# Operand start offsets for each dense stage, and an SSM decay that is spread through a scratch tensor

## The chip, the cores and the metric

One core of one Trainium2 chip runs the whole kernel. The metric is the device time of one execution in microseconds (us), the median of several executions. The engines are PE (TensorE: matmuls, with PEld as its weight loads), DVE (VectorE), ACT (ScalarE), POOL (GpSimd) and SP (SyncE); POOL and SP only issue transfers here.

## The reference

256 tokens of width 1024 in fp32 go through two blocks. The first has one layer: an input projection, a Mamba-2 (SSM) mixer in chunks of 128 beside a gated linear recurrence (LRU), gates, an output projection and a gated FFN. The second has two layers: a projection, three attention-like mixers and an MLP.

```python
cs = cumsum(dA, chunk axis)                       # dA = dt * A, 32 heads, 2 chunks of 128
lmat = exp(cs_i - cs_j) for i >= j else 0         # within a chunk, per head
y_diag = einsum('bcgls,bcgrls,bcsgrp->bclgrp', C B^T, lmat, x*dt)
decay_states = exp(cs_last - cs)                  # carries chunk 0 into chunk 1
...
h = h + (g_ssm * y_ssm + g_lru * y_lru) @ w_out
h = h + (silu(gate) * up) @ w_ffn_out             # gate, up = rmsnorm(h) @ w_ffn_in
# second block, layer l = 0, 1
x = x + concat(retention, dsa, dilated)(rmsnorm(x) @ w_in) @ w_out
x = x + square(relu(rmsnorm(x) @ w_up)) @ w_down
```

## The kernel before

**Dense stages.** Every weight matrix is streamed from HBM once, in transfers of about 1 MB on SP's queue into `raw` (three buffers). Each piece of 128x1024 numbers is split into an upper part `hi` (ACT, L253) and a rest `lo` (DVE, L254), five buffers of each; `next_piece` asks for splits four pieces ahead of use. The activations are split in the same way into a pair of tiles, and each product is three matmuls that add into one PSUM bank (`mm3`, L330 to L332). In `run_a` the weights are the stationary operand (128 columns) and the activations the moving one (256 columns). `run_b` (L380 to L382) turns this round for a few matrices: activations stationary, 512 (at the end 256) columns of `hi` or `lo` moving. A piece of `run_a` is 24 matmuls.

**The stages, by their activation pair.** `xnh`/`xnl` are one pair of buffers that six stages use in turn: "in" (the input projection, 1848 matmuls), "ffn" (1056), "mix0" (384, and 144 of `run_b`), "up0" (768), "mix1" (384 and 144) and "up1" (768). Inside "in" run the output projections of the SSM (`sTh`/`sTl`, 384), of the LRU (`lTh`/`lTl`, 240) and, after the gates, of the block (`mx0`, `mx1`, 192). The others are `ah`/`al` (FFN output, 528), `mxh`/`mxl` (mixer output, 192 for each of the two layers), `mah0`/`mal0` (MLP output of layer 0, 768) and `mah1`/`mal1` (of layer 1, by `run_b`: 288 of 512 columns, 192 of 256).

**Order.** Side work (SSM, LRU, attention, norms) is written as generators; `tick` runs the next step of one after each pair of output tiles of a dense piece. The recording layer then places the instructions of each engine by its own estimates of time, and each engine runs its list strictly in order.

**The decay.** `dt_task` makes `cs`, the cumulative sums of 32 heads, and its two-part split `csp` (L609, L610). For each pair of heads (16 pairs, four to a group `g`), `bc` broadcasts two rows of `cs` over 128 partitions with two matmuls of 256 columns (L669: `idr` is a stacked identity, one column of it repeated), ACT turns the PSUM bank into decay factors `M` with six 128x128 activations (L674, L676) and one 128x512 exponential (L677), and DVE multiplies by `cbT` (L678). `pvm` then multiplies `M` with the tokens (L688). `M` has two buffers. Around it LRU gates run: `lg_run` fills two `ps_sc` banks by matmul, ACT reads them with sigmoids (L777, L778), and the next two banks can be filled only then.

## Time and profile before

| | |
|---|---|
| median of 3 runs | 1210.4 us (1210.18 to 1211.16) |
| profiled execution, its own time | 1216.44 us |
| its span in the trace | 1214.7 us |
| PE busy | 1202.6 us (99%) |
| DVE busy | 846.8 us (70%) |
| ACT busy | 700.5 us (58%) |
| granted TensorE clock, mean | 0.998 of full speed |

The profiled execution took 6.0 us more than the median, and 1.7 us of its time lie outside the span. Matmuls overlap in the pipeline, so that PE shows busy throughout; what tells is how far apart the matmuls of a stretch start.

### The profile page before, as it was taken

The numbers are of one execution on the slowest core, as the hardware profiler recorded it, in microseconds if no ns is written. First come the engines' busy times: TensorE is split into PE (matmuls) and PEld (weight loads), VectorE is DVE, ScalarE is ACT, GpSimd is POOL, SyncE is SP. The second block draws the span as 40 slices with busy tenths as digits, with TensorE's granted clock in tenths as the row PEclk, the third lists the DMA queues.
The fourth block names the chain that finished last, engine by engine and source line by source line (L and its number), as shares of the span: only waits on it lengthen the run. The fifth ranks groups of instructions, "written<-read, shape, count | busy, mean of one in ns | idle before, by whom it ended". The sixth has DMA issues, their size and how long they took to land.

```text
span 1214.7 us, 22653 instructions
## 1 busy us (share of the span) xinstructions
PE 1202.6 (99%) x9369; PEld 1133.3 (93%) x9369; DVE 846.8 (70%) x1483; ACT 700.5 (58%) x1071; POOL 4.6 (0%) x12
## 2 busy tenths in 40 slices
PE   8999999999999999999999999999999999999997
PEld 8999999999999999999897899999997969999886
DVE  7888988987686666557967586655479586666453
ACT  7698788767466444444546575544355376655342
POOL 0000000000000000000000000000000000000000
PEclk9999999999999999999999999999999999999999
DMA  8455444656555655545353455555554434565550
GB/s 299 135 176 172 151 145 150 206 175 204 196 177 177 197 182 178 185 159 194 121 178 105 138 175 179 196 182 183 169 163 143 134 105 158 185 194 175 192 189 35
DMA packets 109382, 205.21 MB, mean 169 GB/s; under 512 B 5792, under 2 KB 15776, under 8 KB 109152
## 3 DMA queue, kind: packets, MB, share of 16 engines
q1 hardware_dynamic: 108560, 201.09, 50.9%
q0 software_dynamic: 576, 2.62, 0.6%
q8 instruction: 73, 1.20, 0.4%
q14 instruction: 29, 0.24, 0.1%
q10 hardware_dynamic: 144, 0.07, 0.0%
HBM read 202.71 MB, written 1.05 MB: 168 GB/s over the span
## 4 chain that ended last, share of the span: by engine, by line
PE 94%; DVE 4%; ACT 1%; DMA 0%; issue 0%; SPq 0%; ACTq 0%
PE ps_mm L330 25%; PE ps_mm L332 25%; PE ps_mm L331 25%; PE ps_mm L380 3%; PE ps_mm L382 3%; PE ps_mm L381 3%; PE ps_sc L327 2%; PE ps_o L1123 1%; PE ps_o L688 1%; DVE lo L254 1%; DVE acc L1069 1%; PE ps_tp L1110 1%; DVE m L1068 1%; PE ps_sc L669 1%; PE ps_tp L941 0%; DMA xt<-in_x 0%
## 5 line engine op out<-in xcount | busy, mean ns | idle before, releaser
L254 DVE TENSOR_TENSOR lo<-raw,hi 128x1024 fp32r<-128x1024 f32 (+2 forms) x382 | 461.9, 1213 | 284.5 <-ACT hi L253 281.4
L253 ACT ACTIVATE hi<-raw 128x1024 fp32r<-128x1024 f32 (+2 forms) x382 | 400.6, 1053 | 425.9 <-PE ps_mm L331 332.5
L330 PE MATMUL ps_mm<-xnh,hi 128*128 128x256 f32 x1736 | 492.4, 284 | 0.0
L331 PE MATMUL ps_mm<-xnl,hi 128*128 128x256 f32 x1736 | 490.3, 283 | 0.0
L332 PE MATMUL ps_mm<-xnh,lo 128*128 128x256 f32 (+1 forms) x1736 | 489.2, 282 | 0.0
L330 PEld LDWEIGHTS ps_mm<-xnh,hi 128*128 128x128 f32 x1736 | 327.9, 189 | 3.8 <-issue 2.5
L331 PEld LDWEIGHTS ps_mm<-xnl,hi 128*128 128x128 f32 x1736 | 329.2, 190 | 1.3 <-DVE xnl L487 0.2
L332 PEld LDWEIGHTS ps_mm<-xnh,lo 128*128 128x128 f32 (+1 forms) x1736 | 328.2, 189 | 0.4 <-issue 0.2
L330 PE MATMUL ps_mm<-mah,hi 128*128 128x256 f32 x256 | 71.9, 281 | 0.0
L331 PE MATMUL ps_mm<-mal,hi 128*128 128x256 f32 x256 | 71.9, 281 | 0.0
L332 PE MATMUL ps_mm<-mah,lo 128*128 128x256 f32 x256 | 71.9, 281 | 0.0
L382 PE MATMUL ps_mm<-hi,mal 128*128 128x256 f32 (+1 forms) x160 | 56.2, 351 | 0.0
L381 PE MATMUL ps_mm<-lo,mah 128*128 128x256 f32 (+1 forms) x160 | 55.9, 349 | 0.0
L380 PE MATMUL ps_mm<-hi,mah 128*128 128x256 f32 (+1 forms) x160 | 55.7, 348 | 0.0
L330 PE MATMUL ps_mm<-ah,hi 128*128 128x256 f32 x176 | 49.2, 280 | 0.0
L331 PE MATMUL ps_mm<-al,hi 128*128 128x256 f32 x176 | 49.2, 280 | 0.0
L332 PE MATMUL ps_mm<-ah,lo 128*128 128x256 f32 x176 | 49.2, 280 | 0.0
L331 PEld LDWEIGHTS ps_mm<-mal,hi 128*128 128x128 f32 x256 | 49.2, 192 | 0.0
L330 PEld LDWEIGHTS ps_mm<-mah,hi 128*128 128x128 f32 x256 | 48.1, 188 | 0.0
L332 PEld LDWEIGHTS ps_mm<-mah,lo 128*128 128x128 f32 x256 | 48.1, 188 | 0.0
L380 PE MATMUL ps_mm<-hi,xnh 128*128 128x512 f32 x96 | 39.1, 407 | 0.0
L382 PE MATMUL ps_mm<-hi,xnl 128*128 128x512 f32 x96 | 37.8, 394 | 0.0
(384 smaller groups left out, 1885.1 us busy)
## 6 DMA issues: line engine op xcount, KB each, us to landing
raw<-in_w_in SPq DMA_DIRECT2D x61, 1024.0 KB, 5.1
raw<-in_w_up SPq DMA_DIRECT2D x32, 1024.0 KB, 5.4
raw<-in_w_down SPq DMA_DIRECT2D x32, 1024.0 KB, 5.0
raw<-in_w_ffn_in SPq DMA_DIRECT2D x22, 1024.0 KB, 5.2
raw<-in_w_ffn_out SPq DMA_DIRECT2D x10, 1024.0 KB, 5.1
...
raw<-in_w_out SPq DMA_DIRECT2D x16, 512.0 KB, 3.8
...
```

What stands on the lines that cost most here:

```text
L253: S.activation(hi, raw, AF.Copy)
L254: V.tensor_sub(lo, raw, hi.bitcast(F32))
L327: PE.matmul(o, w, x_, start=True, stop=True)
L330: PE.matmul(ps, wh, xh, start=start, stop=False, skip_group_check=True)
L331: PE.matmul(ps, wh, xl, start=False, stop=False, skip_group_check=True)
L332: PE.matmul(ps, wl, xh, start=False, stop=stop, skip_group_check=True)
L380: PE.matmul(o, xh[:, ts], hi[:, k, cs], start=st, stop=False, skip_group_check=True)
L381: PE.matmul(o, xh[:, ts], lo[:, k, cs], start=False, stop=False, skip_group_check=True)
L382: PE.matmul(o, xl[:, ts], hi[:, k, cs], start=False, stop=sp, skip_group_check=True)
L669: PE.matmul(o, idr[:, hh:hh + 1].to_broadcast([64, 128]), csp, start=(i == 0), stop=True, skip_group_check=True)
L688: PE.matmul(ps[64 * i:64 * i + 64, c], xtok[g][:, b, (2 * j + i) * 64:(2 * j + i) * 64 + 64], M[:, i, m], start=(j % 2 == 0 and b == 0), s ...
L1068: V.max(m8, acc[:, a:b])
```

## The change

**Offsets.** Every activation pair is now allocated 32 elements too long (`PAD`), and the data begin at an offset of its own, the same for the upper and the lower tile (`OFF`, in elements of 4 bytes). Before, only `xnh`/`xnl` had offsets (`XOFF`). The address that the allocator gives each tile and this offset together set where the operand starts, modulo 128 bytes. In the built programs the weights `hi` and `lo` start at 32 in both, `sTh`, `lTh`, `mx0`, `mx1` and their lower tiles at 96 in both, and the pairs that the change touches start as follows:

| stage (pair) | before | now |
|---|---|---|
| in (`xnh1`) | 32 | 80 |
| ffn (`xnh3`) | 0 | 88 |
| FFN output (`ah`) | 64 | 88 |
| mix0 (`xnh5`) | 0 | 96 |
| mixer output, both layers (`mxh`) | 32 | 104 |
| up0 (`xnh8`) | 96 | 72 |
| MLP output 0 (`mah0`) | 96 | 80 |
| mix1 (`xnh10`) | 32 | 112 |
| up1 (`xnh13`) | 48 | 104 |
| MLP output 1 (`mah1`, stationary) | 64 | 32 |

**Decay.** `dt_task` writes three rows of `cs` (chunk 1, chunk 0, chunk 1) for all heads into a DRAM tensor `csd` from POOL's queue. `decay_load(q)` reads the 768 numbers of a pair of heads from there into all 128 partitions of `M` (384 KB written). Three loads are issued at once, each later one at the end of a `pvm`; `M` has three buffers. `bc` works on `M` in place. The 32 broadcast matmuls, `idr` and `csp` are gone.

```diff
-XOFF = ((8, 24), (0, 16), (32, 48), (56, 72), (72, 88), (12, 28))
+OFF = {"in": (20, 20), "ffn": (22, 22), "mix0": (24, 24), "up0": (18, 18), "mix1": (28, 28), "up1": (26, 26),
+       "ah": (6, 6), "mx": (18, 18), "mah0": (28, 28), "mah1": (24, 24)}
+PAD = 32
...
+    def pair_tiles(pool, k, stage, names, tags=(None, None)):
+        ab = []
+        for n, t, o in zip(names, tags, OFF[stage]):
+            kw = dict(tag=t) if t else {}
+            tl = pool.tile([128, k * T + PAD], F32R, name=n, **kw)
+            ab.append(tl[:, o:o + k * T].rearrange("p (k t) -> p k t", t=T))
+        return ab
...
+    def decay_load(q):
+        if q < 16:
+            Ms[q] = p1.tile([128, 2, 384], F32, tag="M", bufs=MB, name=f"M{q}")
+            P.dma_start(Ms[q].rearrange("p a b -> p (a b)"),
+                        bass.AP(tensor=csd.tensor, offset=csd.offset + 768 * q, ap=[[0, 128], [1, 768]]))
...
+        for r_, b in enumerate((1, 0, 1)):
+            P.dma_start(csd[:, r_, :], cs[:, b, :])
+        for q in range(MB):
+            decay_load(q)
...
         def bc(j):
-            ps = scb()
-            M = p1.tile([128, 2, 384], F32, tag="M", bufs=2, name=f"M{g}{j}")
+            M = Ms[4 * g + j]
             for i in range(2):
                 hh = 8 * g + 2 * j + i
-                o = ps[:, i * 256:i * 256 + 256]
-                PE.matmul(o, idr[:, hh:hh + 1].to_broadcast([64, 128]), csp, start=(i == 0), stop=True,
-                          skip_group_check=True)
-            for i in range(2):
-                hh = 8 * g + 2 * j + i
-                for r_, src, col in ((0, 128, 1), (128, 0, 0)):
-                    S.activation(M[:, i, r_:r_ + 128], ps[:, i * 256 + src:i * 256 + src + 128], AF.Relu,
+                for r_, col in ((0, 1), (128, 0)):
+                    S.activation(M[:, i, r_:r_ + 128], M[:, i, r_:r_ + 128], AF.Relu,
                                  bias=cst[:, col, hh:hh + 1], scale=-1.0)
-                S.activation(M[:, i, 256:384], ps[:, i * 256 + 128:i * 256 + 256], AF.Exp, bias=cst[:, 2, hh:hh + 1])
+                S.activation(M[:, i, 256:384], M[:, i, 256:384], AF.Exp, bias=cst[:, 2, hh:hh + 1])
...
-        ah = pf.tile([128, 22, T], F32R, name="ah")
-        al = pf.tile([128, 22, T], F32R, name="al")
+        ah, al = pair_tiles(pf, 22, "ah", ("ah", "al"))
```

On PE, between the first two `pvm` of group 0, the rows before were (`ps_o` is `pvm`'s bank, the other rows are the dense stage "in"):

```order
L688 MATMUL ps_o_1367<-M_1252,xtok_1186 64x256 x2
L688 MATMUL ps_o_1367<-M_1252,xtok_1186 64x128 x2
L669 MATMUL ps_sc_1372<-csp,idr 128x256 x2
L330 MATMUL ps_mm_1350<-xnh_118,hi_1170 128x256
L331 MATMUL ps_mm_1350<-xnl_119,hi_1170 128x256
```

At the same place of the changed kernel PE has these (L333 and L334 are the lines that were L330 and L331):

```order
L694 MATMUL ps_o_1365<-M_588,xtok_1192 64x256 x2
L694 MATMUL ps_o_1365<-M_588,xtok_1192 64x128 x2
L333 MATMUL ps_mm_1348<-xnh_120,hi_1176 128x256
L334 MATMUL ps_mm_1348<-xnl_121,hi_1176 128x256
L335 MATMUL ps_mm_1348<-xnh_120,lo_1177 128x256
```

The pair of L669 is gone, as the 15 others are; the dense matmuls around it keep their order.

ACT's list before, early in "in", where it splits weights (L253) and evacuates the first LRU tiles (`ut`, `uh`), the first SSM tiles (`xsf`) and the first two gate banks (`rt`, `it`):

```order
L253 ACTIVATE hi_798<-raw_656 128x1024
L621 ACTIVATE xsf_707<-ps_mm_708,pv 128x256
L253 ACTIVATE hi_842<-raw_656 128x1024
L486 ACTIVATE uh_703<-ut_682 128x512
L621 ACTIVATE xsf_707<-ps_mm_709,pv 128x256
L777 ACT_TABLE_LOAD
L777 ACTIVATE rt_863<-ps_sc_849,pv 128x256
```

And now (L256 is the split, L635 the evacuation, L681 and L683 work on the first `M`):

```order
L256 ACTIVATE hi_804<-raw_662 128x1024
L681 ACTIVATE M_588<-M_588,cst 128x128 x2
L635 ACTIVATE xsf_713<-ps_mm_714,pv 128x256
L683 ACT_TABLE_LOAD
L683 ACTIVATE M_588<-M_588,cst 128x128
L681 ACTIVATE M_588<-M_588,cst 128x128 x2
L635 ACTIVATE xsf_713<-ps_mm_715,pv 128x256
L256 ACTIVATE hi_848<-raw_662 128x1024
L493 ACTIVATE uh_709<-ut_688 128x512
L784 ACT_TABLE_LOAD
L784 ACTIVATE rt_869<-ps_sc_855,pv 128x256
```

Five of the first `M`'s activations, which stood behind the first use of the tokens at 96 us, now stand ahead of `hi_848`, `uh_709` and the gates, with a table load of their own. Over the whole program ACT's list has 41 table loads where it had 33.

POOL's list held nothing but the constants' load `c` and what follows it; ahead of that now stand, with the semaphores that each waits for:

```order
L621 DMA csd<-cs 32x128 [waits DVE_49] x2
L621 DMA csd<-cs 32x128
L594 DMA M_588<-csd 128x768 [waits DMASW2_49,DMASW1_49,DMASW0_49]
L594 DMA M_590<-csd 128x768
L594 DMA M_592<-csd 128x768
L594 DMA M_1370<-csd 128x768 [waits DMASW3_49,DVE_49,PE_49]
L594 DMA M_1397<-csd 128x768 [waits DMASW4_49,DVE_49,PE_49]
```

Each load waits for the three stores to have landed, and from the fourth on for PE to have read the buffer that it fills.

## Rows read from the trace of the kernel before

**Rows 1.** The page: busy time by engine, and the last chain by engine.

```profile
PE 1202.6 (99%) x9369; PEld 1133.3 (93%) x9369; DVE 846.8 (70%) x1483; ACT 700.5 (58%) x1071; POOL 4.6 (0%) x12
PE 94%; DVE 4%; ACT 1%; DMA 0%; issue 0%; SPq 0%; ACTq 0%
```

**Rows 2.** PE windows inside single stages: us, busy (matmuls), granted clock, DMA share, GB/s.

```profile
326.00:346.00 20.00, 20.00 (x169) 1.00 0.61 205
348.00:368.00 20.00, 20.00 (x179) 1.00 0.60 188
701.00:708.00 7.00, 7.00 (x64) 1.00 0.42 141
715.00:790.00 75.00, 75.00 (x639) 1.00 0.56 185
794.00:880.00 86.00, 86.00 (x733) 1.00 0.55 180
372.00:495.00 123.00, 123.00 (x1042) 1.00 0.58 186
497.00:557.00 60.00, 60.00 (x514) 1.00 0.55 182
1050.00:1115.00 65.00, 65.00 (x551) 1.00 0.59 188
```

**Rows 3.** The same for `run_b`, 512 columns: mix0, mix1, MLP output 1.

```profile
600.00:610.00 10.00, 10.00 (x45) 1.00 0.55 188
920.00:930.00 10.00, 10.00 (x46) 1.00 0.37 107
1120.00:1160.00 40.00, 40.00 (x173) 1.00 0.56 191
```

**Rows 4.** PE's timeline around one pair of broadcast matmuls: start, duration, instruction.

```profile
99.97 0.28 PE L332 MATMUL ps_mm<-xnh,lo 128*128 128x256 f32 x1
100.18 0.49 PE L669 MATMUL ps_sc<-csp,idr 64*128 64x256 f32 x2
100.61 0.38 PE L330 MATMUL ps_mm<-xnh,hi 128*128 128x256 f32 x1
100.83 0.28 PE L331 MATMUL ps_mm<-xnl,hi 128*128 128x256 f32 x1
```

**Rows 5.** ACT's groups by line and shape: busy, mean ns of one.

```profile
L674 ACT ACTIVATE M<-ps_sc,cst 128x128 f32<-128x128 f32 x64 | 20.3, 379 | 4.4 <-PE ps_sc L669 4.2
L1098 ACT ACTIVATE lgd<-lgd,mmxd 128x128 f32<-128x128 f32 x16 | 6.3, 397 | 0.7 <-DVE mmxd L1096 0.6
L676 ACT ACT_TABLE_LOAD x4 | 5.1, 1283 | 0.0
```

**Rows 6.** When `cs` is ready, on DVE.

```profile
53.40 0.72 DVE L606 TENSOR_TENSOR_SCAN cs<-onew,daT 64x128 f32<-64x128 f32 x2
```

**Rows 7.** Issue time on POOL, then transfers: KB, us from issue to landing.

```profile
L1018 POOL DMA_DIRECT2D uk<-in_dsa_w_uk x2: 538/540/541, 289.9 to 616.8; - x2
out<-xr SPq DMA_DIRECT2D x4, 256.0 KB, 2.2
fw<-in_rows POOLq DMA_DIRECT2D x1, 512.0 KB, 4.7
```

**Rows 8.** ACT and PE around the first gate banks.

```profile
60.51 1.06 ACT L253 ACTIVATE hi<-raw 128x1024 fp32r<-128x1024 f32 x1 [0.85 <-PE ps_mm L331]
67.47 0.47 ACT L777 ACTIVATE rt<-ps_sc,pv 128x256 f32<-128x256 f32 x1
68.00 0.19 PEld L330 LDWEIGHTS ps_sc<-uh,hi 128*128 128x128 f32 x1 [0.25 <-ACT rt L777]
```

**Rows 9.** PE's `pvm` and broadcast matmuls of group 0.

```profile
105.10 0.87 PE L688 MATMUL ps_o<-M,xtok 128*64 128x256 f32 x8
108.76 0.50 PE L669 MATMUL ps_sc<-csp,idr 64*128 64x256 f32 x2
```

**Rows 10.** The stage "in": PE, PEld, DVE, ACT, POOL busy (instructions), clock, DMA, GB/s.

```profile
12.00:300.00 288.00, 287.64 (x2370) 275.49 (x2370) 247.72 (x409) 227.67 (x373) 2.27 (x4) 1.00 0.54 177
```

More of the change, by code (lines that the diff above doesn't have):

```diff
@@ L52 @@
 FM, QM, UM = (2, 3), (0, 0), (2, 3)
-XOFF = ((8, 24), (0, 16), (32, 48), (56, 72), (72, 88), (12, 28))
+OFF = {"in": (20, 20), "ffn": (22, 22), "mix0": (24, 24), "up0": (18, 18), "mix1": (28, 28), "up1": (26, 26),
+       "ah": (6, 6), "mx": (18, 18), "mah0": (28, 28), "mah1": (24, 24)}
+PAD = 32
+STAGES = ("in", "ffn", "mix0", "up0", "mix1", "up1")
 CT = {"ident": 0, "tri": 128, "dup": 512}
@@ L127, in _build @@
     pp = ctx.enter_context(tc.tile_pool(name="pp", bufs=1, space=PSUM))
+    dp = ctx.enter_context(tc.tile_pool(name="dp", bufs=1, space=bass.MemoryType.DRAM))
     V, S, P, PE = nc.vector, nc.scalar, nc.gpsimd, nc.tensor
@@ L404, in _build @@
     xn_s = [0]
+    def pair_tiles(pool, k, stage, names, tags=(None, None)):
[5 more added lines that the diff above has]
+        return ab
     def xn_tiles():
-        offs = XOFF[xn_s[0]]
+        xn_n[0] += 1
+        stage = STAGES[xn_s[0]]
         xn_s[0] += 1
-        xn_n[0] += 1
-        ab = []
-        for k, o in zip("hl", offs):
-            t = cp.tile([128, 8 * T + 112], F32R, tag=f"xn{k}", name=f"xn{k}{xn_n[0]}")
-            ab.append(t[:, o:o + 8 * T].rearrange("p (k t) -> p k t", t=T))
-        return ab
+        return pair_tiles(cp, 8, stage, (f"xnh{xn_n[0]}", f"xnl{xn_n[0]}"), ("xnh", "xnl"))
     def opnd(pair):
@@ L541, in _build @@
             S.activation(h[:, f:f + 2, :].rearrange("p a b -> p (a b)"), hb[f // 2], AF.Copy)
-        idr = cp.tile([64, 32], F32R, name="idr")
-        V.tensor_add(idr, ident[0:64, 0:32], ident[0:64, 32:64])
     p1x = ExitStack()
@@ L575, in _build @@
     cst = p1.tile([128, 3, 32], F32, name="cst")
-    csp = p1.tile([64, T], F32R, name="csp")
+    csd = dp.tile([32, 3, 128], F32, name="csd")
     bcT = p1.tile([128, 8, T], F32, name="bcT")
@@ L580, in _build @@
     S.activation(nega, ssr[:, 32:64], AF.Exp)
+    Ms = {}
+    MB = 3
+    def decay_load(q):
[3 more added lines that the diff above has]
+                        bass.AP(tensor=csd.tensor, offset=csd.offset + 768 * q, ap=[[0, 128], [1, 768]]))
     def dt_task(bdt):
-        raw = p1.tile([32, T], F32, name="dtraw")
+        raw = p1.tile([64, T], F32, tag="dtr", name="dtraw")[:32, :]
         S.activation(raw, bdt[:32, :T], AF.Copy)
@@ L592, in dt_task @@
         softplus(spx, 74, "d")
[L593 to L596 removed]
+        da = p1.tile([128, 2, 32], F32, name="da")
+        V.scalar_tensor_tensor(da, dt, -1.0, nega[:, None, :].to_broadcast([128, 2, 32]), op0=OP.mult, op1=OP.mult)
         V.tensor_scalar(lsc, lsc, -8.0, None, op0=OP.mult)
@@ L600, in dt_task @@
         for b in range(2):
-            PE.transpose(ps[:64, b * 128:b * 128 + 128], da[:, b, :], ident)
-        cs = p1.tile([64, 3, 128], F32, name="cs")
-        daT = p1.tile([64, T], F32, name="daT")
-        V.tensor_copy(daT, ps[:64, :T])
+            PE.transpose(ps[:32, b * 128:b * 128 + 128], da[:, b, :], ident)
+        cs = p1.tile([32, 3, 128], F32, name="cs")
+        daT = p1.tile([64, T], F32, tag="dtr", name="daT")[:32, :]
+        V.tensor_copy(daT, ps[:32, :T])
         for b in range(2):
-            V.tensor_tensor_scan(cs[:, b, :], onew, daT[:, b * 128:b * 128 + 128], 0.0, op0=OP.mult, op1=OP.add)
+            V.tensor_tensor_scan(cs[:, b, :], onew[:32, :], daT[:, b * 128:b * 128 + 128], 0.0, op0=OP.mult, op1=OP.add)
+        for r_, b in enumerate((1, 0, 1)):
+            P.dma_start(csd[:, r_, :], cs[:, b, :])
+        for q in range(MB):
+            decay_load(q)
         V.tensor_scalar(cs[:, 2, :], cs[:, 0, :], cs[:, 0, 127:128], -1.0, op0=OP.subtract, op1=OP.mult)
-        csf = cs[:, 0:2, :].rearrange("p a b -> p (a b)")
-        S.activation(csp, csf, AF.Copy)
-        V.tensor_sub(csp[32:64, :], csf[32:64, :], csp[32:64, :].bitcast(F32))
         yield from pause("dt_task3", 2)
@@ L684, in pvm @@
             ps = obank[0][:, (j % 2) * 256:(j % 2) * 256 + 256]
-            M = Ms.pop(j)
+            M = Ms.pop(4 * g + j)
             for b, c, m in ((0, slice(0, 256), slice(128, 384)), (1, slice(128, 256), slice(0, 128))):
@@ L692, in pvm @@
                 V.tensor_add(dst, dst, obank[0].rearrange("p (a b) -> p a b", b=T))
+            decay_load(4 * g + j + MB)
         bc(0)
@@ L878, in mix_tiles @@
         xn_n[0] += 1
-        return (pool.tile([128, 8, T], F32R, name=f"mxh{xn_n[0]}"), pool.tile([128, 8, T], F32R, name=f"mxl{xn_n[0]}"))
+        return pair_tiles(pool, 8, "mx", (f"mxh{xn_n[0]}", f"mxl{xn_n[0]}"))
     class Norm:
```

9 lines of the change are left out of this document (1 added, 8 removed).

## The prediction

> **What bounds the kernel now.** I read the page first: PE is busy for 1202.6 of 1214.7 us and carries 94% of the chain that ended last, while DVE and ACT are at 70% and 58% [rows 1]. So time is saved only where PE's matmuls come closer together, where some go, or where PE stops waiting. "Busy" does not show how close they are, since one matmul runs into the next; therefore windows that lie inside single stages, where the number of matmuls is the measure. A window also counts the two that are under way at its edges: 20 us with 169 is 20/167 = 119.8 ns from start to start [rows 2]. The reader is to see that equal matmuls (128x128 weights, 256 moving columns, full granted clock) are not equally far apart, and that the distance goes with the start of the moving operand modulo 128 bytes, with the weights at 32 throughout:
>
> - 32 ("in", 326 to 346 us): 119.8 ns
> - 0 ("ffn", 372 to 495): 118.3
> - 64 (FFN output, 497 to 557): 117.2
> - 48 ("up1", 1050 to 1115): 118.4
> - 96: 113.0 in the block's output projection (348 to 368) and 112.9 at the start of "up0" (701 to 708), but 117.7 in the rest of "up0" (715 to 790) and 117.6 in MLP output 0 (794 to 880) [rows 2].
>
> So 96 has two paces, about 113.0 (call it A) and 117.7 (B), with the same operands: "up0" runs in A until its norm's small matmuls break the stream, and in B from there on, as does the stage behind it. Where the roles are turned and 512 columns move from 32, the pair 0/32 (activations/weights) takes 232.6 ns, 32/32 takes 227.3 and 64/32 takes 233.9 [rows 3].
>
> **The change, offsets.** No instruction is added here; the term is a number of matmuls times a difference of pace. No row has a start at 72, 80, 88, 104 or 112, so I bound them by the nearest rows, the two paces of 96: 113.0 below, 117.7 above. For 72 to 96 I take 114.6, which is two parts A and one B, since "in" and its neighbours return again and again from breaks and the row at 96 in that part of the program is at 113.0. For 104 and 112, which lie on the way to 0 (118.3 and no A), I take the middle, 115.3. Then, in us:
>
> - in: 1848 x (119.8 - 114.6) = 9.6
> - ffn: 1056 x (118.3 - 114.6) = 3.9; FFN output: 528 x (117.2 - 114.6) = 1.4
> - mix0, which was at 0 as ffn: 384 x 3.7 = 1.4; mix1, which was at 32 as in: 384 x (119.8 - 115.3) = 1.7; mixer outputs, also from 32: 2 x 192 x 4.5 = 1.7
> - up0: the 704 of 768 that are in B: 704 x (117.7 - 114.6) = 2.2; MLP output 0: 768 x (117.6 - 114.6) = 2.3; up1: 768 x (118.4 - 115.3) = 2.4
> - MLP output 1 goes from 64/32 to 32/32: 288 x (233.9 - 227.3) = 1.9; its 192 of 256 columns I leave at nothing
> - `run_b` of mix0 and mix1 (144 each): 0/32 becomes 96/32 and 32/32 becomes 112/32. With 227.3 and 233.9 as bounds the first is left at nothing, the second loses half of 6.6 ns, 0.5.
>
> Together 28.0 us; all in A gives 40.4, all in B 7.3. The added 32 elements, and the other tiles' shift, cost no instruction.
>
> One rule speaks against this whole part. The Trainium skill, in "TensorE: Matmul & The Clock Gate", section "Step-by-step: what each phase is for", says that TensorE has two independent read ports into SBUF, one for the moving operand and one for the weights. By it, where the one starts against the other could not matter and this term would be zero. The rows at 32 and at 96 differ by 6.8 ns with the same shapes, weights' start and clock, so they decide against it here.
>
> **The change, decay.** Gone are 16 pairs of L669. From the dense matmul ahead of a pair to the second one behind it, 0.86 us pass (99.97 to 100.83), where two dense ones need 0.24: a pair costs 0.62 us [rows 4], 16 pairs 9.9 us. `csp` and `idr` are a microsecond of ACT and DVE beside PE's work: nothing.
>
> Against that, the first wait. `cs` is ready at 53.40 + 0.72 = 54.1 us [rows 6]. Three stores at 0.54 us of issue each end at 55.7; the store row takes 2.2 us to land, so 57.9. The load needs 0.54 of issue and 4.7 to land, by the row of the same queue and form (one DRAM row into all partitions): 63.2 us [rows 7]. With 2.2 for both it would be 60.6, with 4.7 for both 65.7. ACT comes to the first `M` when its split ends, at 60.51 + 1.06 = 61.6 [rows 8]; it waits 1.6 us (0 to 4.1). Then stand, ahead of the gates, five activations at 0.4 and a table load of 1.28 that were not there: 3.3 us [rows 5]. Queued behind them are a split, `uh` and the sigmoids, and PE already waits for the last of these now, 0.25 us before 68.00 [rows 8]. So 1.6 + 3.3 = 4.9 us come on PE there; 2.4 if ACT's idle 0.85 covers its share and the load is in time, 7.4 at the other end.
>
> ACT has 8 table loads more. One is counted; seven are 9.0 us [rows 5], and its 96 activations read SBUF instead of PSUM, 397 for 379 ns by the nearest row, 1.7 us. ACT has room (227.7 of 288 us in "in") [rows 10], and weights are split four pieces ahead, 96 matmuls or 11 us, so only loads ahead of a side result that PE waits for reach PE: I take 2 us, between 0 and 9.0.
>
> The fourth load of each group is late too. It can start when `pvm` is done, 105.10 + 0.87, and lands 5.2 us later, at 111.2 [rows 7, 9]; the work of the fourth pair follows 108.8. ACT waits some 2.2 us, four times. The 11 us of split weights hide it: nothing, at most 8.8.
>
> So the decay is worth 9.9 - 4.9 - 2 = 3.0 us, between 7.5 gained and 15.3 lost. 6 MB more traffic meets a DMA share of 0.54 [rows 10] and is free.
>
> Last, DVE: 247.7 us of work in "in" now fill 288 us [rows 10], then about 275, 90%. Side chains keep their length while the matmuls that cover them shrink; I take 1 us of new waits.
>
> **Sum.** 28.0 + 3.0 - 1 = 30.0 us. The profiled execution's 1216.4 becomes 1186.4; it stood 6.0 above the median, so the median goes from 1210.4 to 1180.4, say 1180. About 0.2%, 2.4 us, is what a measurement of this kernel can tell from no change.
>
> **The rivals.**
>
> - *Pace A everywhere.* For it: both rows in which a stream at 96 begins show A. Against it: the two long rows at 96 show B. 40.4 + 3.0 - 1: 1168 us. Chance 0.22.
> - *Pace B everywhere*, because each break of the stream picks B, as the one in "up0" did. 7.3 + 3.0 - 1: 1201 us. Chance 0.19.
> - *ACT takes the decay's gain and more.* The table loads and the late `M` all come on PE: 28.0 - 15.3 - 1: 1199 us. For it speaks PE's wait at 68 us, against it ACT's 21% of idle time. Chance 0.09.
> - *The offset does nothing*, the pace belongs to the stage and its neighbours: 3.0 - 1, 1208 us. Against it: "in" at 119.8 lies right beside 113.0 in rows 2. Chance 0.03. The two read ports of the Trainium skill ("TensorE: Matmul & The Clock Gate", section "Step-by-step: what each phase is for") would give this too.
> - *Slower: the starts that no row shows are worse than 32.* The 6824 matmuls of 256 columns that move now average 118.7 ns; the other terms leave 3.4 us, so at 119.2 nothing is won, and at 121 the time is 1223 us. Against it: no row of the dense stages is above 119.8, and 72 to 88 lie between starts that are all below. Chance 0.07.
>
> The forecast itself has 0.40, with 1172 to 1190 as its own range. 1164 to 1203 takes in A with a little more gain, B and the ACT case, and leaves out the last two and the far end of A. Faster by over 0.2% come out the first four cases but for the edge of B: 0.87; within 0.2% 0.06; slower 0.07.
>
> **What would show it.** Windows inside the stages: "in" at 113 to 118 ns instead of 119.8 is the first thing to look at, MLP output 1 at 227 the next. No broadcast matmul between dense ones. At about 65 us, ACT in front of its first `M` waiting for a load, and PE waiting for a sigmoid some microseconds later; 41 table loads. The sum is wrong if a new start has a pace outside 113 to 118, if the breaks choose otherwise than two to one, or if PE's waits in "in" add up to much more than 7 us.

## The result, and the profile after

The change made the kernel slower. Its median is 1222.7 us (4 runs, 1222.2 to 1224.9) against 1210.3 for the kernel before (4 runs); the ratio of the times is 1.0104, with a 95% interval from 1.0087 to 1.0122. The forecast was 1180, its range 1164 to 1203.

One thing about the measure first. The kernel before has two levels: in one batch of 16 runs of it 9 lie at 1210.0 to 1210.6 and 7 at 1216.4 to 1216.8, and in the other batches both appear too. The execution read ahead of the prediction was one of the upper level (1216.4). Below, times are therefore compared as medians with their ranges, and those of before by the level meant.

The page of the changed kernel (span and busy time; the granted TensorE clock in 40 slices; the chain that ended last, by engine):

```profile
span 1220.8 us, 22649 instructions
PE 1200.0 (98%) x9337; PEld 1134.0 (93%) x9337; DVE 846.7 (69%) x1480; ACT 713.2 (58%) x1078; POOL 14.7 (1%) x31
PEclk9989999999999999999999999999999999999999
PE 85%; DVE 7%; ACT 3%; DMA 2%; issue 2%; SPq 0%; POOL 0%; DVEq 0%; POOLq 0%; ACTq 0%
```

PE is as busy as before although 32 matmuls are gone [rows 1]; the chain has less PE and more of DVE, ACT and DMA; and the clock has a dip in the third slice (61 to 92 us) that before did not have.

Windows inside the dense stages, to be read as [rows 2] (time over the count less two):

```profile
326.00:346.00 20.00, 20.00 (x172) 20.00 (x171) 13.62 (x21) 10.37 (x15) 0.00 (x0) 1.00 0.55 182
350.00:370.00 20.00, 20.00 (x172) 20.00 (x171) 14.73 (x23) 12.05 (x19) 0.00 (x0) 1.00 0.60 196
376.00:496.00 120.00, 120.00 (x1007) 120.00 (x1006) 78.46 (x93) 57.86 (x68) 0.00 (x0) 1.00 0.57 184
500.00:560.00 60.00, 60.00 (x503) 60.00 (x502) 30.43 (x31) 26.15 (x32) 0.00 (x0) 1.00 0.53 176
720.00:794.00 74.00, 74.00 (x619) 74.00 (x618) 48.56 (x52) 40.76 (x53) 0.00 (x0) 1.00 0.53 178
800.00:880.00 80.00, 80.00 (x682) 80.00 (x681) 38.42 (x37) 32.93 (x36) 0.00 (x0) 1.00 0.55 180
1050.00:1115.00 65.00, 65.00 (x544) 65.00 (x543) 41.50 (x45) 36.07 (x48) 0.00 (x0) 1.00 0.57 186
1127.00:1167.00 40.00, 40.00 (x175) 32.73 (x174) 18.29 (x17) 15.90 (x16) 0.00 (x0) 1.00 0.58 193
```

| stage | start before, after | ns before | ns after |
|---|---|---|---|
| in (326 to 346) | 32, 80 | 119.8 | 117.6 |
| output projection (350 to 370) | 96, 96 | 113.0 | 117.6 |
| ffn | 0, 88 | 118.3 | 119.4 |
| FFN output | 64, 88 | 117.2 | 119.8 |
| up0 | 96, 72 | 117.7 | 119.9 |
| MLP output 0 | 96, 80 | 117.6 | 117.6 |
| up1 | 48, 104 | 118.4 | 119.9 |
| MLP output 1 (512 columns) | 64, 32 | 233.9 | 231.2 |

So "in" won 2 ns, the stages at 72, 88 and 104 lost 1 to 3, and the output projection, which the change does not touch, lost its 113. No new start shows 113, and MLP output 1 won 2.7 ns where 6.6 were forecast.

Where the decay comes in, PE waits. Its largest group of waits between 40 and 200 us (total, times, longest):

```profile
PE ps_sc L333 <- ACT rt L784: 7.3, 2, 5.2
```

ACT of the changed kernel in order of time (start, duration, what; in brackets the idle time ahead and what ended it; three rows between 68 and 70 us are left out):

```profile
59.84 1.06 ACT L256 ACTIVATE hi<-raw 128x1024 fp32r<-128x1024 f32 x1 [0.41 <-PE ps_mm L334]
64.76 0.69 ACT L681 ACTIVATE M<-M,cst 128x128 f32<-128x128 f32 x2 [3.85 <-DMA M<-csd]
65.36 0.55 ACT L635 ACTIVATE xsf<-ps_mm,pv 128x256 f32<-128x256 f32 x1
65.93 1.28 ACT L683 ACT_TABLE_LOAD   x1
67.22 0.40 ACT L683 ACTIVATE M<-M,cst 128x128 f32<-128x128 f32 x1
67.53 0.68 ACT L681 ACTIVATE M<-M,cst 128x128 f32<-128x128 f32 x2
70.14 1.28 ACT L784 ACT_TABLE_LOAD   x1
71.44 0.47 ACT L784 ACTIVATE rt<-ps_sc,pv 128x256 f32<-128x256 f32 x1
```

This is the picture that the prediction drew: ACT idle in front of its first `M`, a table load and five activations, then a second table load, and only then the sigmoid on which PE waits. PE in order of time on both sides of that wait:

```profile
67.06 0.28 PE L335 MATMUL ps_mm<-xnh,lo 128*128 128x256 f32 x1
67.18 0.28 PE L333 MATMUL ps_mm<-xnh,hi 128*128 128x256 f32 x1
72.69 0.58 PE L333 MATMUL ps_sc<-uh,hi 128*128 128x256 f32 x1 [5.23 <-ACT rt L784]
73.07 0.41 PE L334 MATMUL ps_sc<-ul,hi 128*128 128x256 f32 x1
73.28 0.41 PE L335 MATMUL ps_sc<-uh,lo 128*128 128x256 f32 x1
```

Equal matmuls start 0.12 us apart ahead of it and 0.21 behind it: the clock has gone from 2.4 to 1.2 GHz. Two windows of the changed kernel show it behind the two waits for a gate (the third number from the end is the granted clock), and two shorter ones the stretches in which PE ran again and the clock was still low:

```profile
70.00:90.00 20.00, 17.31 (x132) 17.31 (x133) 15.35 (x26) 19.08 (x32) 0.00 (x0) 0.83 0.31 104
170.00:190.00 20.00, 18.27 (x144) 18.27 (x145) 14.48 (x31) 18.62 (x32) 0.00 (x0) 0.91 0.33 111
72.70:76.60 3.90, 3.90 (x18) 3.90 (x19) 3.00 (x6) 3.09 (x7) 0.00 (x0) 0.50 0.45 135
172.30:175.60 3.30, 3.30 (x18) 3.30 (x17) 2.38 (x6) 2.80 (x6) 0.00 (x0) 0.50 0.58 214
```

At half the clock PE loses half of the 3.9 + 3.3 us, 3.6 in all. (The 0.83 and 0.91 of the long windows would give 5.2, but the first of them also counts a stretch, 70 to 72.7 us, in which PE was waiting anyway.)

### The profile page after: what moved, and what is told of

It is laid out like the page before. It is cut to its first block, busy times and chain, and to the rows that moved or that the text cites. A ratio compares the mean times of both kernels' runs of the same rounds, so it can differ in the third digit from the quotient of the medians.

```text
span 1220.8 us, 22649 instructions
## 1 busy us (share of the span) xinstructions
PE 1200.0 (98%) x9337; PEld 1134.0 (93%) x9337; DVE 846.7 (69%) x1480; ACT 713.2 (58%) x1078; POOL 14.7 (1%) x31
## 4 chain that ended last, share of the span: by engine, by line
PE 85%; DVE 7%; ACT 3%; DMA 2%; issue 2%; SPq 0%; POOL 0%; DVEq 0%; POOLq 0%; ACTq 0%
PE ps_mm L333 23%; PE ps_mm L334 23%; PE ps_mm L335 22%; PE ps_mm L383 3%; PE ps_mm L385 3%; PE ps_mm L384 3%; DVE lo L257 2%; PE ps_sc L330 2%; PE ps_o L1129 1%; DMA M<-csd 1%; DVE acc L1075 1%; PE ps_tp L1116 1%; ACT hi L256 1%; DVE m L1074 1%; PE ps_o L694 1%
## 5 line engine op out<-in xcount | busy, mean ns | idle before, releaser
L256 ACT ACTIVATE hi<-raw 128x1024 fp32r<-128x1024 f32 (+2 forms) x382 | 399.7, 1050 | 413.2 <-PE ps_mm L334 318.8
L333 PE MATMUL ps_mm<-xnh,hi 128*128 128x256 f32 x1736 | 491.7, 284 | 0.0
L334 PE MATMUL ps_mm<-xnl,hi 128*128 128x256 f32 x1736 | 489.8, 282 | 0.1
L333 PEld LDWEIGHTS ps_mm<-xnh,hi 128*128 128x128 f32 x1736 | 328.8, 190 | 3.3 <-issue 2.7
L334 PEld LDWEIGHTS ps_mm<-xnl,hi 128*128 128x128 f32 x1736 | 327.4, 189 | 1.6 <-issue 0.3
L334 PE MATMUL ps_mm<-mal,hi 128*128 128x256 f32 x256 | 71.9, 281 | 0.0
L333 PE MATMUL ps_mm<-mah,hi 128*128 128x256 f32 x256 | 71.8, 281 | 0.0
L333 PE MATMUL ps_mm<-ah,hi 128*128 128x256 f32 x176 | 49.9, 284 | 0.0
L334 PE MATMUL ps_mm<-al,hi 128*128 128x256 f32 x176 | 49.7, 282 | 0.0
L333 PEld LDWEIGHTS ps_mm<-mah,hi 128*128 128x128 f32 x256 | 48.7, 190 | 0.0
L334 PEld LDWEIGHTS ps_mm<-mal,hi 128*128 128x128 f32 x256 | 48.1, 188 | 0.0
```

The lines of the kernel that those rows point to most:

```text
L256: S.activation(hi, raw, AF.Copy)
L333: PE.matmul(ps, wh, xh, start=start, stop=False, skip_group_check=True)
L334: PE.matmul(ps, wh, xl, start=False, stop=False, skip_group_check=True)
```

## The experiments

The first theory was that the starts had been given the wrong paces and that the decay costs time by itself; the rivals put all of the loss on one of the two halves.

**The offsets alone.** The new table `OFF` and `pair_tiles`, the decay as before.

> The kernel of before with the new starts of the dense operands alone; the decay is still spread by PE. Theory (the starts took the paces wrongly and the decay costs time by itself): the new starts win 1 to 3 us in "in" and lose as much or more behind it, and the output projections lose their pace of 113 ns: 1207 to 1216 us. Rival (the decay alone is at fault, the starts are worth the forecast's 28 us): 1182 us. Second rival (the starts alone are at fault): 1220 us or more.

Measured: 1222.6 us (1222.5 to 1223.7). The offsets alone give the whole loss, as the second rival said; the theory's figure was 7 us too low. That the changed kernel takes the same time does not make its decay free: the two programs differ in one thing more, the weights, which stand 128 bytes further on here, and the untouched projections run slower for it. What is left for the decay is worked out at the end.

**The decay alone.** The decay's part of the diff, and smaller pads to make room:

```diff
-XOFF = ((8, 24), (0, 16), (32, 48), (56, 72), (72, 88), (12, 28))
+XOFF = ((8, 8), (0, 0), (0, 0), (24, 24), (8, 8), (12, 12))
-            t = cp.tile([128, 8 * T + 112], ...)
+            t = cp.tile([128, 8 * T + 32], ...)
```

> The kernel of before with the decay spread through the scratch tensor alone; every dense operand starts as in before modulo 128 bytes (the pads are cut to make room). Theory (PE's 7.3 us of waits for the gates and the clock's two falls behind them outweigh the 9.9 us of broadcast matmuls that go): 1212 to 1220 us, with the clock below 1.00 right behind each long wait for a gate. Rival (the forecast's sum for the decay, 3.0 us gained): 1207 us and no fall of the clock.

Measured: 1212.0 us (1210.7 to 1213.3). The time is at the edge of the theory's, but the clock falls to 0.83 and 0.91 in the same two windows, as it said. The next run shows what it must be compared with.

**The smaller pads alone.** Only the two lines above: every operand keeps its start modulo 128, but the second tile of a pair and the weights move against the first by odd multiples of 128 bytes.

> The kernel of before with smaller pads of the normed inputs and nothing else: every operand of every matmul keeps its start modulo 128 bytes, and most move by whole multiples of 128 bytes. Theory (the pace belongs to the start modulo 128 bytes, or to nothing that the addresses decide): within 0.2% of before, 1208 to 1213 us, with 113 ns in the output projections. Rival (pace 113 hangs on the exact addresses or on chance): the projections at 117 to 118 and some 2 to 6 us more.

Measured: 1217.9 us (1217.8 to 1218.1), and the projection ran at 18/153 = 117.6 (a window, as above):

```profile
350.00:368.00 18.00, 18.00 (x155) 18.00 (x154) 14.33 (x24) 11.88 (x19) 0.00 (x0) 1.00 0.55 176
```

The theory fell: the start modulo 128, on which the whole dense term rested, does not fix the pace. The run with the decay is 5.9 us below this one, but its matmuls are also closer together, for its weights stand 128 bytes away from those of this run. In "in" it has 20/170 = 117.6 ns and this run 20/167 = 119.8 (with the decay first):

```profile
326.00:346.00 20.00, 20.00 (x172) 20.00 (x171) 13.80 (x21) 10.52 (x16) 0.00 (x0) 1.00 0.50 170
326.00:346.00 20.00, 20.00 (x169) 20.00 (x169) 13.67 (x22) 10.35 (x15) 0.00 (x0) 1.00 0.51 163
```

By the spacing of the matmuls over whole stages the run with the decay has 117.7 for 119.6 in "in" (1848 matmuls), 113.4 for 117.8 in the block's output projection (192) and MLP output 0 (768), and 117.1 for 118.5 in ffn (1056): 3.5 + 0.8 + 3.4 + 1.5 = 9.2 us. So it is not the decay that wins the 5.9 us; the decay takes some 3 us.

**Matmuls alone, 16 starts in steps of 8 bytes.** A kernel of dense matmuls only; the sets are

```python
def quiet(o, w):      # 96 matmuls; both tiles of the pair start at o
    brk()             # small transposes
    for j, t, k in ...:
        mm3(ps, hi, lo, xf_h[:, o + ...], xf_l[:, o + ...])
```

> Dense matmuls alone: 96 of them (256 moving columns, accumulating) for each of the 16 starts of the moving operand in steps of 8 bytes, twice in different orders, with small matmuls between any two sets; first with weights that stay in SBUF at 32 and nothing else running, then four starts with the weights at 64, 96 and 0, then all 16 twice with weights that come by DMA and are split by ACT and DVE as in the real kernel. It computes no part of the reference's output. Theory (the start is not what sets the pace, or hardly): all 16 within 2 ns of each other in the quiet part, and in the loaded part 117 to 120 with no order by start. Rival (the start sets it): the same start shows the same pace in both orders, 32 is the slowest near 120, and 72 to 96 lie at 113 to 118. Second rival (two paces of which the break picks one): sets at 113 and sets at 118 for one and the same start.

Measured, mean ns from start to start, weights at 32 modulo 128, the two tiles an odd multiple of 128 bytes apart (the mean of two sets a start; gaps above 150 ns left out):

```
start          0      16     32     48     64     80     96     112
quiet        118.0  117.6  118.6  118.0  118.4  117.8  117.7  118.7
streamed     117.4  117.8  117.8  117.8  118.5  117.8  117.8  117.8
start          8      24     40     56     72     88     104    120
quiet        120.6  120.9  120.8  120.6  119.8  119.8  120.1  120.2
streamed     120.7  120.8  120.4  121.1  118.0  119.5  120.4  120.3
```

The theory fell. Of the rival, the same start does give the same pace in both orders, to 0.4 ns in the quiet part, but 32 is not the slowest, and no set came to 113, so that the second rival's two paces did not show either. (With the weights at 64, 96 and 0, the starts 0, 32, 64 and 96 gave 117.8 to 118.9.) Here is the first cause: a start that is 8 modulo 16 costs about 1.5 to 3 ns a matmul (72 with streamed weights excepted). Every start in the trace of before was a multiple of 16, so no row could show it, and five of the changed stages (ffn and its output at 88, up0 at 72, up1 and the mixer outputs at 104) are off that grid.

**The changed kernel, put on the grid.**

```diff
-OFF = {"in": (20, 20), "ffn": (22, 22), "mix0": (24, 24), "up0": (18, 18), "mix1": (28, 28), "up1": (26, 26),
-       "ah": (6, 6), "mx": (18, 18), "mah0": (28, 28), "mah1": (24, 24)}
+OFF = {"in": (20, 20), "ffn": (24, 24), "mix0": (24, 24), "up0": (20, 20), "mix1": (28, 28), "up1": (28, 28),
+       "ah": (8, 8), "mx": (20, 20), "mah0": (28, 28), "mah1": (24, 24)}
```

> The changed kernel with only those stages moved whose start is 8 modulo 16 bytes: ffn and its output from 88 to 96, up0 from 72 to 80, up1 and the mixer outputs from 104 to 112. Theory (a start off the 16-byte grid costs about 2 ns a matmul): 1056 x 1.7 + 528 x 2.2 + 768 x 2.0 + 768 x 2.4 + 384 x 2 = 7.1 us less than 1222.7, so 1215 to 1217 us, with 117.8 to 118.5 ns in these stages. Rival (these stages' paces have another cause): 1222 to 1223 us.

Measured: 1215.9 us (1210.7 to 1217.4), 6.8 less than the changed kernel. The profiled execution was the fastest; its windows in ffn, FFN output, up0 and up1:

```profile
376.00:492.00 116.00, 116.00 (x988) 116.00 (x987) 76.93 (x91) 56.09 (x65) 0.00 (x0) 1.00 0.58 186
496.00:556.00 60.00, 60.00 (x512) 60.00 (x511) 31.10 (x33) 26.85 (x33) 0.00 (x0) 1.00 0.53 178
720.00:790.00 70.00, 70.00 (x608) 70.00 (x607) 47.25 (x51) 39.02 (x50) 0.00 (x0) 1.00 0.58 190
1040.00:1105.00 65.00, 65.00 (x555) 65.00 (x554) 42.54 (x47) 37.16 (x49) 0.00 (x0) 1.00 0.59 192
```

117.6, 117.6, 115.5 and 117.5 ns: the theory holds. In up0 and, behind it, in MLP output 0 one start in three came 113 to 114 ns after the one before, all through the stages, and the others 116 and 117.5: 115.6 on average, where MLP output 0 of the changed kernel, with the same starts, had 117.6. So these starts have two paces as well, which may be why this kernel's times spread; only one of its executions was traced.

**The changed kernel, its other stages put off the grid.** "in" 20 to 22, mix0 24 to 26, mix1 28 to 30, mah0 28 to 30, mah1 24 to 26.

> The changed kernel with the other stages moved off the 16-byte grid by 8 bytes: "in" from 80 to 88, mix0 from 96 to 104, mix1 from 112 to 120, MLP output 0 from 80 to 88, MLP output 1 from 32 to 40. Theory (a start off the grid costs about 2 to 3 ns a matmul): 1848 x 3 + 768 x 2.7 + 768 x 2.5 = 9.5 us more than 1222.7, so 1230 to 1235 us. Rival (the start does not matter): 1222 to 1223 us.

Measured: 1225.6 us (1225.3 to 1225.9), 2.8 more, between theory and rival. The paces rose ("in" 326 to 346: 20/168 = 119.0; MLP output 0: 80/671 = 119.2),

```profile
326.00:346.00 20.00, 20.00 (x170) 20.00 (x169) 13.76 (x22) 10.36 (x15) 0.00 (x0) 1.00 0.52 166
800.00:880.00 80.00, 80.00 (x673) 80.00 (x672) 38.82 (x38) 32.73 (x36) 0.00 (x0) 1.00 0.52 174
```

By the spacing of the starts the moved stages lost 6.7 us ("in" 3.7 of them), about 2 ns a matmul and less than the theory's 9.5. But all that lies ahead of the output projection grew by 0.7 us alone, and that projection shrank by 0.8 (113.4 again in its 192 matmuls). PE waited less at the gates (6.9 us for 7.3), and the clock stayed at 1.00 in 170 to 190 us, where it was 0.91; that a slower stream waits less is how I read this, and no run tests it.

**Every pair at 96 modulo 128**, the decay as before: all six stages of `xn` to 24, `ah` 8, `mx` 16, `mah0` 0, `mah1` 8.

> The offsets alone (the decay as before), but every pair of dense operands starts at 96 modulo 128 bytes. Theory (a start on the 16-byte grid gives 117.8 ns, and which stages fall into 113.3 is not decided by the start): against the kernel with the changed starts alone (1222.6), ffn, its output, up0, up1 and the mixer outputs win about 2 ns in 3500 matmuls and mixers and "in" stay, 1213 to 1217 us, less by 4.5 ns a matmul for every stage that happens to fall into 113.3. Rival (96 is the start of the pace 113, and stages that all have it keep it): below 1195 us.

Measured: 1211.8 us (1211.6 to 1212.2), a little below the theory's range, and far from the rival. By the spacing of the starts, nearly all of it is at 117.8. 96 alone is not the way to 113.

**The kernel before, profiled again.**

> The kernel of before once more, for a second profile: its times lie at 1210.3 and at 1216.6 us, and the profile read so far was of 1216.4. Theory (some stage at 96 falls into 113.3 ns in one execution and not in the other): an execution at 1210.3 shows 113.3 in up0 or in MLP output 0, some 1400 matmuls by 4.5 ns. Rival (a wait differs): the same paces and a stall of 6 us that is there or not.

This execution took 1216.4 us and told nothing new. A third one:

> The kernel of before a third time, for its profile. If it falls at 1210 us: theory (two levels of one pace), 113.3 ns in up0 behind its first 64 matmuls or in MLP output 0. If it falls at 1216 us, it tells nothing new.

It took 1210.2 us. Its windows in up0 and MLP output 0:

```profile
715.00:790.00 75.00, 75.00 (x664) 75.00 (x663) 51.47 (x58) 43.76 (x57) 0.00 (x0) 1.00 0.58 188
794.00:874.00 80.00, 80.00 (x709) 80.00 (x708) 38.65 (x37) 33.81 (x36) 0.00 (x0) 1.00 0.56 186
```

75/662 = 113.3 and 80/707 = 113.2, where the execution of [rows 2] had 117.7 and 117.6. 704 x 4.4 + 768 x 4.4 = 6.5 us: that is the distance of the two levels (6.2 us between these two executions). One program runs in pace A or in B there, and what falls out at the break behind up0's first 64 matmuls differs from execution to execution: B in the two traces of 1216.4 us, A in this one.

**The relation modulo 256.** Read from the programs' addresses, all stages that ran at 113 in before have both tiles at 224 modulo 256 and the weights at 32 modulo 256. The added 32 elements (128 bytes) of the changed kernel put the two tiles of a pair 128 bytes apart modulo 256; in the run with the offsets alone the weights stand at 160 besides. So every pair was set to 224 with both tiles, the decay as before (the last two lines against `pair_tiles` of the changed kernel):

```diff
+OFF = {"in": (56, 0), ... all of xn ..., "ah": (0, 0), "mx": (0, 0), "mah0": (0, 0), "mah1": (0, 0)}
+POST = {"in": 40, ... , "ah": 56, "mx": 16, "mah0": 0, "mah1": 56}
-            tl = pool.tile([128, k * T + PAD], ...)
+            tl = pool.tile([128, k * T + o + post * (n == names[1])], ...)
```

> The offsets alone (the decay as before): every pair of dense operands, both tiles of it, starts at 224 modulo 256 bytes, with the weights at 32 modulo 256, which is how the output projections stand in the kernel of before, where they run at 113.3 ns. In the kernels run so far the added 32 elements set the two tiles of a pair 128 bytes apart modulo 256. Theory (113.3 needs both tiles of the pair and the weights in this relation modulo 256): the stages fall into 113.3 wherever the stream is not broken, 6800 matmuls by up to 4.5 ns below the 1211.8 of all pairs at 96: 1180 to 1200 us. Rival (the relation modulo 256 does not matter, 113.3 is chance): 1205 to 1213 us.

Measured: 1188.4 us (1187.1 to 1192.0), 22 us below the lower level of before. Its windows in ffn, FFN output, up0 and MLP output 0:

```profile
372.00:484.00 112.00, 112.00 (x990) 112.00 (x989) 75.25 (x88) 56.91 (x65) 0.00 (x0) 1.00 0.61 196
488.00:544.00 56.00, 56.00 (x497) 56.00 (x496) 29.27 (x31) 25.97 (x31) 0.00 (x0) 1.00 0.55 184
695.00:772.00 77.00, 77.00 (x681) 77.00 (x680) 52.69 (x63) 43.77 (x59) 0.00 (x0) 1.00 0.61 199
776.00:858.00 82.00, 82.00 (x726) 82.00 (x725) 41.34 (x40) 35.13 (x39) 0.00 (x0) 1.00 0.56 191
```

113.4, 113.1, 113.4 and 113.3 ns. Not all of it came: "in" is at 114.9 by the spacing of its starts, and the output projection, which was at 113 in the kernel before with the same starts, ran at 18/153 = 117.6:

```profile
344.00:362.00 18.00, 18.00 (x155) 18.00 (x155) 13.63 (x22) 10.22 (x16) 0.00 (x0) 1.00 0.55 180
```

**The weights 128 bytes further**, which modulo 128 is the same kernel (`POST` of the `xn` stages 40 to 72):

> As the run with every pair at 224 modulo 256, but with all split weights 128 bytes further on: 160 modulo 256. Modulo 128 bytes the two are the same. Theory (the distance between moving operand and weights modulo 256 decides): 117.8 ns everywhere, in the output projections too, 1211 to 1215 us. Rival (the moving operand's own start decides): the same time as with the weights at 32.

Measured: 1210.7 us (1210.1 to 1211.3). Its windows in ffn and up1:

```profile
376.00:494.00 118.00, 118.00 (x1005) 118.00 (x1004) 77.26 (x92) 57.41 (x67) 0.00 (x0) 1.00 0.58 188
1030.00:1104.00 74.00, 73.99 (x652) 73.87 (x651) 50.15 (x60) 44.25 (x61) 0.00 (x0) 1.00 0.60 192
```

117.6 in ffn, and 117.4 to 117.8 by the spacing in all other stages, as the theory said, but 113.8 in up1: the relation makes 113 rare, not impossible.

**The second tile 128 bytes further**, weights at 32 (`OFF` of the `xn` stages (56, 0) to (56, 32), `POST` 40 to 8):

> The run with every pair at 224 modulo 256 (decay by PE), with one edit: the second tile of the normed inputs begins 128 bytes later, so it stands at 96 modulo 256 and the first at 224. All starts are 96 modulo 128 as before. Theory (113.3 needs both tiles of the pair in the same relation to the weights): 117.8 ns in "in", ffn, up0, up1 and the mixers, 113.3 still in the FFN output, the mixer outputs and MLP output 0, about 18 us more than 1188.4: 1203 to 1208 us. Rival (the first tile's relation is enough): 1187 to 1192 us.

Measured: 1210.2 us (1209.9 to 1211.4), more than the theory's range. Its windows in up0 and MLP output 0:

```profile
703.00:787.00 84.00, 84.00 (x717) 84.00 (x716) 56.49 (x67) 47.60 (x63) 0.00 (x0) 1.00 0.58 188
791.00:877.00 86.00, 86.00 (x733) 86.00 (x732) 41.09 (x40) 35.34 (x39) 0.00 (x0) 1.00 0.54 180
```

117.5 in up0, whose pair is split, and 117.6 in MLP output 0, whose pair is not: it follows up0 without a break and has its pace, as the FFN output has that of ffn. (That a stage takes over the pace of the one ahead is not a rule: in the run with the decay alone MLP output 0 was at 113.4 directly behind an up0 at 117.8.) The rival is out: a second tile 128 bytes off is enough to lose 113, and that is what the pad of 32 elements does.

**Matmuls alone over 512 bytes**, both tiles of the pair at the same start, weights fixed at 32 modulo 256 (two passes, the second with no break between sets):

> Dense matmuls alone, with both tiles of the pair at the same start, in 32 steps of 16 bytes over 512 bytes, and the weights fixed at 32 modulo 256: 96 matmuls a start, first with small matmuls between any two sets, then once more in another order without a break. It computes no part of the reference's output. Theory (the relation modulo 256 decides): the same picture in both halves of the 512 bytes, about 113.3 near 224 in at least one of the two passes, 117 to 120 at 32, 0 and 128 and 117.8 or more at 96. Rival (nothing beyond 16 bytes matters): 117 to 119 for all 32.

Measured, mean ns, by the start modulo 256; four sets each, both halves of the 512 bytes:

```
  0: 118.3 x4                    128: 120.0 120.1 120.0 120.0
 16: 117.2 x4                    144: 113.6 113.6 113.8 113.6
 32: 119.9 119.9 120.0 119.9     160: 118.6 118.6 118.7 118.7
 48: 116.6 116.6 116.7 118.7     176: 118.7 118.7 118.6 118.6
 64: 117.8 117.8 116.7 116.7     192: 117.3 117.3 117.3 118.7
 80: 118.4 118.3 118.3 118.4     208: 119.2 119.3 119.2 119.2
 96: 117.8 113.3 117.8 113.3     224: 113.4 117.8 113.4 117.8
112: 120.0 119.9 120.0 120.0     240: 119.1 119.2 119.1 119.1
```

No weights stream in here and no side work runs, so that the starts of the two operands alone make these differences. The pace repeats with 256 bytes and not with 128 (16 and 144 differ by 3.6 ns), it agrees with [rows 2] where those stages stand modulo 256 ("in" 32: 119.8; ffn 0: 118.3; FFN output 192: 117.2; up0 224: 112.9 and 117.7; up1 48: 118.4, as one of the four sets there), and 224 and 96 have two paces each. 144 has one, and it is 113.6. What picks one of the two paces, the starts do not say. The theory's 117.8 or more at 96 fell.

**The decay on top.** Every pair at 224, and the decay by transfers:

> Every pair at 224 modulo 256 with the weights at 32, as above, and the decay spread through the scratch tensor. Theory (the decay by transfers is worth 0 to 1 us in "in", since PE's waits for the gates and the clock's falls behind them take what the broadcast matmuls gave): within 2 us of the run with every pair at 224 and the decay by PE. Rival (the decay costs, as the wait at the gates suggests): 3 to 8 us more; second rival (it is worth the forecast's 3 us): 3 us less.

Measured: 1196.2 us (1193.7 to 1199.4), 7.9 more than with the decay by PE: the rival. PE's largest group of waits in 40 to 200 us:

```profile
PE ps_sc L333 <- ACT rt L785: 8.5, 2, 5.7
```

**ACT's work on `M` held back**, the transfers untouched. One DVE instruction a group makes the biases of `M` wait for the group's finished `xsf`:

```diff
+        cg = cst[:, :, 8 * g:8 * g + 8]
+        V.scalar_tensor_tensor(cg, xsf[:, 0, 0:24]..., 0.0, cg, op0=OP.mult, op1=OP.add)
```

> Every pair at 224 modulo 256 and the decay by transfers, but the activations on M can no longer be placed ahead of the gates: a small addition of zero times the group's xs makes their biases wait for it. The transfers stay as they are. Theory (what PE loses is ACT's work on M and its table loads, which stand ahead of the sigmoids that PE waits for, and the clock's fall behind that wait): PE's longest wait for rt falls from 5.7 us to under 1, the clock stays at 1.00 in 70 to 90 us, 1188 to 1191 us. Rival (the transfers themselves cost it, by their traffic): 1195 us or more, as the run with the same decay unheld.

Measured: 1186.5 us (1184.4 to 1192.5), 9.7 less. All that is left of PE's waits for the gates in 40 to 200 us:

```profile
PE ps_sc L333 <- ACT rt L787: 0.2, 1, 0.2
```

And its window from 70 to 90 us, with the clock at 1.00:

```profile
70.00:90.00 20.00, 20.00 (x171) 19.95 (x170) 16.92 (x25) 19.90 (x28) 0.00 (x0) 1.00 0.49 166
```

The wait and the clock are as the theory said, and the time is a little below its range; the transfers as such cost nothing that shows.

**The same in the changed kernel:**

> The changed kernel with the activations on M held back in the same way, and nothing else. Theory (ACT's early work on M makes PE wait, 7.3 us and two falls of the clock): 4 to 8 us less than 1222.7. Rival (the dense stages alone make the changed kernel slow, and PE's waits are covered): 1221 to 1223 us.

Measured: 1215.4 us (1214.8 to 1216.1), 7.4 less than 1222.7. Its window from 70 to 90 us, without the fall of the clock:

```profile
70.00:90.00 20.00, 20.00 (x175) 20.00 (x175) 16.79 (x28) 19.91 (x31) 0.00 (x0) 1.00 0.44 147
```

**Every pair at 144**, decay held back: `OFF = {"xn": (36, 28), "ah": (4, 12), "mx": (4, 36), "mah0": (4, 20), "mah1": (4, 12)}`, each pair in one tile.

> As the run with every pair at 224 modulo 256 and the held decay (1186.5 us), with the pairs of normed inputs, FFN hidden, mixer outputs and MLP hidden at 144 modulo 256 (each pair in one tile), weights at 32; the output projections stay at 224. Theory (the pace follows the table of the matmuls alone: 113.6 at 144 in each set, two paces at 224): "in" and the mixers, which stand between the two paces at 224, come to 113.6 to 114.5, ffn and up0 and up1 stay at 113.4 to 113.8, 1178 to 1186 us. Rival (the table does not hold where weights stream in and side work breaks the stream): 117 to 119 ns and 1200 us or more.

Measured: 1185.4 us (1185.3 to 1185.8), the lowest median of all, though the spread of the run with 1186.5 (1184.4 to 1192.5) covers it; its own spread is small. It is 0.975 of before by the runs of its batch, interval 0.972 to 0.978. Its windows in ffn, up0 and MLP output 0:

```profile
368.00:478.00 110.00, 110.00 (x971) 110.00 (x971) 74.28 (x87) 55.88 (x65) 0.00 (x0) 1.00 0.60 195
690.00:767.00 77.00, 77.00 (x681) 77.00 (x680) 52.74 (x63) 43.67 (x58) 0.00 (x0) 1.00 0.61 198
771.00:853.00 82.00, 82.00 (x726) 82.00 (x726) 41.40 (x40) 35.17 (x39) 0.00 (x0) 1.00 0.56 191
```

113.5, 113.4 and 113.3. The output projection, at 224 here, was also at 113.3. The time is at the upper end of the theory's range: MLP output 1, where this pair is the weights, got slower (188.0 ns a matmul on average for 182.8 with every pair at 224, 2.5 us), and the mixers' inputs came to 115.1 and 115.2 by the spacing, above the theory's 114.5.

## Why the prediction was wrong

**The step that failed is the bound on the starts**: "No row has a start at 72, 80, 88, 104 or 112, so I bound them by the nearest rows, the two paces of 96: 113.0 below, 117.7 above." The new starts took 117.6 (80) and 119.4 to 119.9 (72, 88, 104). The bound was broken from above, since all rows lay on a grid of 16 bytes and three of the five unseen starts do not; and nothing came near the bound below. With the paces of the table, "in" wins 1848 x 2.2 = 4.1 us, ffn loses 1.2, its output 1.4, up0 1.5, up1 1.2: these five, forecast at 19.5 of the 28.0, give -1.2. By the spacing of all starts the whole term of 28.0 came to 0.3: the matmuls of 256 columns that move average 118.8 ns, where they had 118.7, and MLP output 1 won 0.8 of its 1.9 us. The rival "the starts that no row shows are worse than 32", held at 0.07, came true in its kind, for some of the starts. That its 1223 us came out as well is luck: they were worked out from 121 ns on average, and the time that was lost came from elsewhere, as follows.

**Beneath it lay a wrong key.** "The distance goes with the start of the moving operand modulo 128 bytes" was read from rows in which two stages at 0 or three at 96 looked alike. The matmuls alone show that the pace repeats with 256 bytes. Modulo 256, both tiles of a pair and the weights must stand right if a stage is to count on 113, and the pad of 32 elements, of which the prediction said that it costs no instruction and which it left at nothing, parts the tiles by 128. With it no new start can count on 113, 96 included. And in the run with the offsets alone it moved the weights to 160, and the untouched projections and LRU gates, some 870 matmuls, ran at 117.8 for 113.7: 3.6 us. In the changed kernel the weights are at 32 again and part of these blocks at 113, but the output projection is not. Why stays open: with the same starts it was at 113 in the kernel before and in the run with the decay alone, behind an "in" at 119.8 and at 117.6, and at 117.6 with every pair at 224.

**The forecast 114.6, "two parts A and one B"**, took A as something that a stage at 96 mostly has. A is a state that a stream enters or not, then keeps until it is broken, in most of the traces over the border of stages too. Which way a break goes is not settled by these runs: with the weights at 32 and the pairs whole most streams went into A, with the weights at 160 nearly none did, and the same program did both.

**The reckoning from the upper level** failed as well: "it stood 6.0 above the median, so the median goes from 1210.4 to 1180.4". Those 6.0 us were pace B in up0 and MLP output 0, not an offset that all executions share; the sum counted 4.5 us as to be won there, which the median of before had already. None of the changed kernel's runs shows that level: 6.3 of the 12.4 us lost are the distance from 1216.6 down to 1210.3. The other 6 us are to be explained from the paces of each run. In the run with the offsets alone (1222.6 against 1216.6) "in" wins 3.8 us by the spacing of its starts, ffn, its output, up0 and up1 lose 6.6, the untouched projections and the gates 3.5, and the other stages win 0.6: 5.7 lost, nearly all of it. In the changed kernel, with the weights at 32, the same sum gives 2.4, so that some 4 us are left there for the decay.

**The decay** was right in its mechanism and in its place, and too small in its price. Its first wait was forecast as 4.9 us on PE and was 5.2, which is in part luck: the first load landed at 64.8 us and not at 63.2, so that ACT waited 3.85 us for it and not 1.6. The two waits for the gates come to 7.3. PE was idle for 288 - 278.9 = 9.1 us between 12 and 300 us, where it had been for 0.4 [rows 10], so that all waits together added 8.7; 6.9 were forecast.

```profile
12.00:300.00 288.00, 278.92 (x2325) 269.32 (x2325) 246.63 (x405) 238.93 (x378) 10.74 (x20) 0.98 0.60 197
```

What was missing is the clock, a term that the forecast left at nothing: at each wait for a gate it fell, and that took 3.6 us more. 8.7 + 3.6 against the 9.9 us that the broadcast matmuls gave is 2.4 lost, where 3.0 gained was the forecast; the paces above leave some 4, and no run shows where the rest went. The Trainium skill, in "TensorE: Matmul & The Clock Gate", section "HAM oscillation — how this bites in real kernels", describes such a fall behind a stall of PE; the trace agrees, with a granted clock of 0.50 when PE went on after 5.2 us of waiting. Held back, the same transfers gave 7.4 us in the changed kernel; unheld they took 7.9 where the dense stages were fast. The guess that late fourth loads and memory traffic cost nothing was not contradicted by any run.

**The rule that was weighed**, two independent read ports (the Trainium skill, "TensorE: Matmul & The Clock Gate", "Step-by-step: what each phase is for"), was put aside rightly: the weights moved by 128 bytes with the moving operands left in place cost 22.3 us (1188.4 to 1210.7). The two streams do meet somewhere; where, no run shows.
